# One-hot tiles of a PEER gate moved from VectorE to GpSimd, and a weight split issued earlier

## The chip, the cores and the metric

The kernel runs on one core of one Trainium2 chip. A core has a matrix engine, TensorE (PE, whose weight loads the profile lists apart as PEld), and three engines for elementwise work: VectorE (DVE), ScalarE (ACT) and GpSimd (POOL). SyncE (SP) issues most DMAs. The metric is the device time of one execution in microseconds (us), lower is better. Before the change three runs gave a median of 2891.4 us, from 2889.86 to 2892.06.

## What is computed

Two decoder blocks on 512 tokens of width 1024, all in float32. The first block is a mixer (sparse attention beside an SSD scan), a cross attention to a memory, and a PEER feed-forward; the second is another mixer and a convolutional feed-forward. The change lies at the end of the cross attention and in PEER. Cut to that:

```python
h = h + memory_cross_attention(...)          # ends with o @ w_o
af = rmsnorm(h, norm_ffn_g)
qry = (af @ w_q).reshape(n, 8, 2, 128)
s = einsum('nhpd,hpkd->nhpk', qry, sub_keys) # two sets of 128 keys per head
s_top, i_top = top_k(s, 16)
cand = s_top[:, :, 0, :, None] + s_top[:, :, 1, None, :]
sc, ci = top_k(cand, 16)
e_a, e_b = (i_top[.., 0] at ci // 16), (i_top[.., 1] at ci % 16)
experts = e_a * 128 + e_b                    # 8 x 16 of 16384 per token
gw = softmax(sc)
act = gelu(einsum('td,tkd->tk', x, u_tab[experts]))
y = einsum('tk,tkd->td', gw * act, v_tab[experts])
```

## The kernel before

Tokens lie in four tiles of 128. PE multiplies in float32 by splitting each operand into a high part in a reduced format and the rest: `wtile` (L166 to L185) loads a weight tile of 128x1024 (`raw`, on SP's queue, L173), ACT copies it rounded (`whi`, L181), DVE subtracts (`wlo`, L184), and `mms` makes three products (L195 to L197). The weight tiles go round a few shared buffers in the order in which they are asked for.

The program is written as plain loops; the Tile scheduler decides the order on each engine, and each engine then runs its list in order. A tile allocated from a pool waits until the last readers of the buffer that it takes are done.

`cross` ends with eight output projections, each added to the residual by DVE (L883). `peer_query` then splits the residual into `fs` (ACT L254, DVE L255), sums squares for the norm (`rms_acc`, DVE and POOL at L276), and makes 16 query projections with the weights `w_pq[m]` through `proj_cm`. After the second of them `normed` finishes the norm (`rms_end`: sums by PE at L284, L287 on DVE, `rstd` on POOL at L289; `rbcast`, L296, on PE). Each query is multiplied with keys, and DVE takes the top 16 of 128 (L928 to L932).

PEER treats token tile 0 and the others differently. For token tile 0 the chosen rows of `u_tab` and `v_tab` are gathered by indirect DMAs that POOL issues (`gather`, L1035) and used by DVE (`sparse_step`, L1047 and L1060). For tiles 1 to 3 every expert is computed densely by PE: `dense_u` makes u for 128 experts of each of 128 rows (L1063 on), `dense_v` sums them up, weighted by a gate matrix that is zero outside the chosen experts.

`peer_route` finds the chosen experts of one token tile (L947 to L1007, all on DVE but an Exp); with its one-hot steps `oh` at L980, L983 and L986 it maps places in the candidate list to indices, and for tiles 1 to 3 it leaves them, transposed, in `eT` (L1006). `gate_chunk` makes the gate matrix of 32 tokens in 8 blocks of four tokens. For a block DVE makes B (L1015: for each token the one-hot of its e_b, 128x512 in one operation), and A holds per token the one-hot of e_a times the weight gw. A is made token by token, j = 0 to 3: some j by two ACT operations (L1021, L1022), as the table GA = ((2, 3), (3,)) says (j = 2 and 3 in even blocks, j = 3 in odd ones), the others by one DVE operation each (L1024). PE multiplies the four pairs (L1027), ACT copies the result to `stg` (L1028), and SP stores it after eight blocks (L1030). There are 12 chunks, so 96 blocks. Each product shows as two records in the trace.

A and B are `wk` tiles, 128x512, and share the six buffers (PTMP = 6) of one pool: three blocks can be made ahead of PE. `peer` issues the work from a list with due places: the route of a token tile, its four chunks, and between them the 64 first `dense_u` (UONLY = 64) and 12 first steps of the gather path. The gathered rows go round six buffers (GB = 6).

## Time and profile before

| | |
|---|---|
| median of 3 runs | 2891.4 us (2889.86 to 2892.06) |
| profiled execution | 2889.49 us, its span 2887.8 us |
| mean granted clock of PE | 0.992 of full speed |
| PE busy | 2815.3 us, 97% of the span |
| DVE busy | 2081.4 us, 72% |
| ACT busy | 1286.3 us, 45% |
| POOL busy | 619.6 us, 21% |

The profile is that of one execution; its times count from the span's start. "Idle" in a row is the time for which an engine had nothing to run before the instruction, and behind an arrow stands what ended it. A share of busy time is an average over the whole span; what a stage could win has to be read in that stage. The gate chunks run from 1110 to about 1385 us, the last sum of the cross attention is at 915.66 us.

### The profile page before, as it was taken

What the parts mean: (1) busy time and instruction counts of PE and PEld (TensorE: products, weight loads), DVE (VectorE), ACT (ScalarE), POOL (GpSimd) and SP (SyncE); (2) the same over time, 40 slices, a digit from 0 to 9 for tenths busy, and PEclk for the clock granted to TensorE, in tenths of its full rate; (3) what the DMA queues carried; (4) which work ended last, traced back from release to release, by engine and by line L of the source; (5) the groups of instructions that cost most, each with busy time, mean ns of one, the idle gap of its engine ahead of it and who ended that gap; (6) DMA issues with size and microseconds to landing.
All of it is one profiled execution on the core that took longest, in us unless ns stands there. A gap on an engine that the chain in (4) does not pass through costs nothing.

```text
span 2887.8 us, 38487 instructions
## 1 busy us (share of the span) xinstructions
PE 2815.3 (97%) x14365; PEld 2407.0 (83%) x14365; DVE 2081.4 (72%) x3721; ACT 1286.3 (45%) x2208; POOL 619.6 (21%) x448
## 2 busy tenths in 40 slices
PE   7899999999999999999999999999999999999998
PEld 6767788888887899999988888888887778888887
DVE  7986874545556999967578787878895876564646
ACT  4256764333434337777433333333333664432322
POOL 3421330001201000000245454554550010010100
PEclk9999999999999999999999999999999999999999
DMA  4211113324423245677899999999992202223332
GB/s 132 81 52 59 52 52 95 96 87 139 138 81 99 88 133 171 207 252 249 281 341 345 332 350 337 346 339 345 334 379 73 95 30 74 88 80 101 96 95 88
DMA packets 179852, 491.98 MB, mean 170 GB/s; under 512 B 14880, under 2 KB 66336, under 8 KB 179472
## 3 DMA queue, kind: packets, MB, share of 16 engines
q1 hardware_dynamic: 142320, 353.97, 36.4%
q0 software_dynamic: 37344, 135.54, 13.4%
q8 instruction: 113, 1.85, 0.3%
q14 instruction: 75, 0.61, 0.1%
HBM read 446.39 MB, written 41.94 MB: 169 GB/s over the span
## 4 chain that ended last, share of the span: by engine, by line
PE 82%; DVE 10%; issue 4%; ACT 2%; POOL 0%; DMA 0%; DVEq 0%; POOLq 0%; ACTq 0%
PE mm L197 10%; PE mm L196 10%; PE mm L195 10%; PE acc L1106 6%; PE acc L1108 6%; PE acc L1112 6%; PE u L195 5%; PE u L196 5%; PE u L197 5%; PE mm L1027 3%; PE mm L1395 2%; PE mm L1397 2%; PE mm L1398 2%; DVE wlo L184 1%; PE sm L303 1%
## 5 line engine op out<-in xcount | busy, mean ns | idle before, releaser
L181 ACT ACTIVATE whi<-raw 128x1024 fp32r<-128x1024 f32 x498 | 526.9, 1059 | 1104.1 <-PE mm L196 348.6
L184 DVE TENSOR_TENSOR wlo<-raw,whi 128x1024 fp32r<-128x1024 f32 x476 | 614.2, 1292 | 387.1 <-ACT whi L181 325.2
L195 PE MATMUL u<-nsh,whi 128*128 128x384 f32 x1024 | 347.6, 339 | 2.7 <-ACT al L1070 2.7
L196 PE MATMUL u<-nsl,whi 128*128 128x384 f32 x1024 | 346.4, 338 | 0.0
L197 PE MATMUL u<-nsh,wlo 128*128 128x384 f32 x1024 | 345.8, 338 | 0.0
L1035 POOL DMA_INDIRECT gr<-u_tab,pidx x128 | 187.3, 1463 | 638.1 <-DVE gr L1047 253.2
L1035 POOL DMA_INDIRECT gr<-v_tab,pidx x128 | 200.2, 1564 | 193.5 <-DVE acc L1060 172.1
L1106 PE MATMUL acc<-whi,Wh 128*128 128x512 f32 x768 | 237.7, 391 | 0.0
L1108 PE MATMUL acc<-whi,Wl 128*128 128x512 f32 x768 | 237.0, 390 | 0.0
L195 PEld LDWEIGHTS u<-nsh,whi 128*128 128x128 f32 x1024 | 193.1, 189 | 5.3 <-ACT al L1070 3.0
L1112 PE MATMUL acc<-wlo,Wh 128*128 128x512 f32 x768 | 194.9, 389 | 0.0
L196 PEld LDWEIGHTS u<-nsl,whi 128*128 128x128 f32 x1024 | 193.0, 188 | 2.3
L197 PEld LDWEIGHTS u<-nsh,wlo 128*128 128x128 f32 x1024 | 192.9, 188 | 0.0
L195 PE MATMUL mm<-ah,whi 128*128 128x512 f32 x424 | 173.3, 409 | 13.4 <-ACT whi L181 13.4
L197 PE MATMUL mm<-ah,wlo 128*128 128x512 f32 x424 | 170.5, 402 | 1.4 <-DVE wlo L184 1.2
L196 PE MATMUL mm<-al,whi 128*128 128x512 f32 x424 | 170.6, 402 | 0.0
L1108 PEld LDWEIGHTS acc<-whi,Wl 128*128 128x128 f32 x768 | 144.1, 188 | 31.4
L1112 PEld LDWEIGHTS acc<-wlo,Wh 128*128 128x128 f32 x768 | 144.1, 188 | 30.0
L1106 PEld LDWEIGHTS acc<-whi,Wh 128*128 128x128 f32 x768 | 143.3, 188 | 26.3
L1060 DVE SCALAR_TENSOR_TENSOR acc<-gr,act,acc 128x1024 f32<-128x1024 f32 x127 | 163.3, 1286 | 1.6
L1047 DVE SCALAR_TENSOR_TENSOR gr<-gr,xt 128x1024 f32<-128x1024 f32 x128 | 152.4, 1219 | 0.0
L196 PE MATMUL mm<-fl,whi 128*128 128x512 f32 (+1 forms) x336 | 129.8, 387 | 0.3
(642 smaller groups left out, 6089.5 us busy)
## 6 DMA issues: line engine op xcount, KB each, us to landing
raw<-uT SPq DMA_DIRECT2D x128, 512.0 KB
raw<-v_tab SPq DMA_DIRECT2D x128, 512.0 KB
raw<-w_cm SPq DMA_DIRECT2D x61, 512.0 KB
gd<-stg SPq DMA_DIRECT2D x12, 2048.0 KB
Gl<-gd SPq DMA_DIRECT2D x32, 768.0 KB
ad<-al SPq DMA_DIRECT2D x32, 384.0 KB
al<-ad SPq DMA_DIRECT2D x16, 768.0 KB
raw<-w_fg SPq DMA_DIRECT2D x22, 512.0 KB
```

Of the source, the lines that this page charges most:

```text
L181: nc.scalar.activation(hi[:, :n], raw[:, :n], AF.Copy)
L184: self.paced = (eng or nc.vector).tensor_tensor(lo[:, :n], raw[:, :n], hi[:, :n].bitcast(F), op=OP.subtract)
L195: mm(ps, w[0][:, cs[k]], xh, start=k0 + k == ends[0], stop=False)
L196: mm(ps, w[0][:, cs[k]], xl, start=False, stop=False)
L197: mm(ps, w[1][:, cs[k]], xh, start=False, stop=k0 + k == k1)
L1027: nc.tensor.matmul(pg[:, j * 128:(j + 1) * 128], B[:, j], A[:, j], start=True, stop=True)
L1035: self.nc.gpsimd.indirect_dma_start(out=t, out_offset=None, in_=self.I[tab], in_offset=bass.IndirectOffsetOnAxis(ap=self.idx[:, j:j + 1], ...
L1047: nc.vector.scalar_tensor_tensor(u, u, 1.0, self.xt, op0=OP.mult, op1=OP.mult, accum_out=self.act0[:, i:i + 1])
L1060: nc.vector.scalar_tensor_tensor(self.acc0, v, w, self.acc0, op0=OP.mult, op1=OP.add)
L1106: mm(self.accp[tt * 2 + hf], wh[:, ts], hi[:, cs[hf]], start=first, stop=False)
L1108: mm(self.accp[tt * 2 + hf], wl[:, ts], hi[:, cs[hf]], start=False, stop=False)
L1112: mm(self.accp[tt * 2 + hf], wh[:, ts], lo[:, cs[hf]], start=False, stop=last)
```

## The change

Two edits. In `gate_chunk` the tile of j = 0 is made by GpSimd with the same operation; j = 1, and j = 2 in odd blocks, stay on VectorE. And the weight `w_pq[0]` is asked for (loaded and split) in the code of `cross`, ahead of the last addition, instead of in `peer_query`.

```diff
@@ cross
         for m in range(8):
             ps = self.proj_cm(I["w_co"][m], os)
+            if m == 7:
+                self.wq = self.wtile(I["w_pq"][0], 1024)
             nc.vector.tensor_tensor(h(m), h(m), ps, op=OP.add)
@@ peer_query
         for m in range(16):
             hd, q = divmod(m, 2)
-            ps = self.proj_cm(I["w_pq"][m], fs)
+            ps = self.proj_cm(I["w_pq"][m], fs, w=None if m else self.wq)
@@ gate_chunk
-                    nc.vector.tensor_scalar(A[:, j], self.io128, e, w, op0=OP.is_equal, op1=OP.mult)
+                    (nc.vector if j else nc.gpsimd).tensor_scalar(A[:, j], self.io128, e, w, op0=OP.is_equal, op1=OP.mult)
```

All lines behind the first edit have numbers higher by 2 in the changed kernel. The scheduler lays the work out anew. Three places of the new order:

POOL, from the preparation of PEER on, in the kernel before (`sa` and `rstd` belong to the norm):

```order
L944 MEMSET grid 128x1152
L276 TENSOR_TENSOR sa_7357<-sa_7357,sq 128x512 x3
L289 TENSOR_TENSOR rstd<-rv,mhalf 128x4
L1035 DMA gr<-u_tab,pidx 128x1024 x128
L1035 DMA gr<-v_tab,pidx 128x1024 x128
```

The same place of the changed kernel:

```order
L946 MEMSET grid 128x1152
L276 TENSOR_TENSOR sa_7363<-sa_7363,sq 128x512 x3
L289 TENSOR_TENSOR rstd<-rv,mhalf 128x4
L1026 TENSOR_SCALAR A<-io_7332,eT 128x128 x32
L1037 DMA gr<-u_tab,pidx 128x1024
L1026 TENSOR_SCALAR A<-io_7332,eT 128x128 x11
L1037 DMA gr<-u_tab,pidx 128x1024 x2
L1026 TENSOR_SCALAR A<-io_7332,eT 128x128 x8
L1037 DMA gr<-u_tab,pidx 128x1024 x2
L1026 TENSOR_SCALAR A<-io_7332,eT 128x128 x8
L1037 DMA gr<-u_tab,pidx 128x1024
L1026 TENSOR_SCALAR A<-io_7332,eT 128x128 x5
```

The gathers stood alone in the queue; now they stand among the one-hot tiles, with up to eleven of these ahead of one.

DVE, up to the fourth block of the fourth chunk (its tiles are A_9993 and B_9994), in the kernel before; `prc`, `pt8` and `oh` belong to the route of the next token tile:

```order
L972 CAST prc_11252<-pcu_11249 128x256
L974 SCALAR_TENSOR_TENSOR pt8_11254<-prc_11252 128x128
L975 TENSOR_TENSOR prc_11252<-prc_11252,pt8_11254 128x128
L976 TENSOR_TENSOR prc_11252<-prc_11252,pt8_11254 128x128
L980 TENSOR_TENSOR oh_11259<-prc_11252,io16_7324 128x2048
L1015 TENSOR_TENSOR B_9994<-io128_7326,eT_7330 128x512
L1024 TENSOR_SCALAR A_9993<-io128_7326,eT_7330 128x128 x3
L1015 TENSOR_TENSOR B_10008<-io128_7326,eT_7330 128x512
```

The same place of the changed kernel:

```order
L982 TENSOR_TENSOR oh_11259<-prc_11252,io16_7330 128x2048
L184 TENSOR_TENSOR wlo_10070<-raw_10066,whi_10068 128x1024
L184 TENSOR_TENSOR wlo_10103<-raw_10099,whi_10101 128x1024
L985 TENSOR_TENSOR oh_11259<-oh_11259,pit_11203 128x2048
L988 TENSOR_TENSOR oh_11259<-oh_11259 128x128x8
L988 TENSOR_TENSOR oh_11259<-oh_11259 128x128x4
L184 TENSOR_TENSOR wlo_10222<-raw_10218,whi_10220 128x1024
L988 TENSOR_TENSOR oh_11259<-oh_11259 128x128x2
L184 TENSOR_TENSOR wlo_10373<-raw_10369,whi_10371 128x1024
L1017 TENSOR_TENSOR B_9994<-io128_7332,eT_7336 128x512
L1026 TENSOR_SCALAR A_9993<-io128_7332,eT_7336 128x128 x2
L1017 TENSOR_TENSOR B_10008<-io128_7332,eT_7336 128x512
```

Ahead of the block there are now four weight splits and the rest of a one-hot step. Counted from the first B of the stage to this one, DVE makes 40 tiles A instead of 67, 13 splits instead of 12, and three times the steps L983 and L986 (L985 and L988 now) instead of twice; all else is the same.

PE at that block, before; the u products are those of `dense_u`:

```order
L1027 MATMUL mm_9987<-A_9978,B_9979 128x128 x4
L195 MATMUL u_10072<-nsh_7377,whi_10068 128x384
L196 MATMUL u_10072<-nsl_7378,whi_10068 128x384
L197 MATMUL u_10072<-nsh_7377,wlo_10070 128x384
L195 MATMUL u_10072<-nsh_7377,whi_10068 128x384
L196 MATMUL u_10072<-nsl_7378,whi_10068 128x384
L197 MATMUL u_10072<-nsh_7377,wlo_10070 128x384
L1027 MATMUL mm_10001<-A_9993,B_9994 128x128 x4
```

And in the changed kernel:

```order
L1029 MATMUL mm_9972<-A_9964,B_9965 128x128 x4
L1029 MATMUL mm_9987<-A_9978,B_9979 128x128 x4
L195 MATMUL u_10072<-nsh_7383,whi_10068 128x384
L1029 MATMUL mm_10001<-A_9993,B_9994 128x128 x4
L196 MATMUL u_10072<-nsl_7384,whi_10068 128x384
L1029 MATMUL mm_10016<-A_10007,B_10008 128x128 x2
```

Five of the six u products ahead of the block stand behind it now.

DVE at the last sum of the cross attention (L883, the second row of hx_62 here), before:

```order
L883 TENSOR_TENSOR hx_62<-hx_62,mm 128x512
L184 TENSOR_TENSOR wlo<-raw,whi 128x1024 x3
L883 TENSOR_TENSOR hx_62<-hx_62,mm 128x512
L341 TENSOR_SCALAR flip<-fp 128x128
L346 TENSOR_TENSOR ix<-ix,ip 128x128
```

The changed kernel, there and up to the first top-16 step (L930 now):

```order
L885 TENSOR_TENSOR hx_62<-hx_62,mm 128x512
L184 TENSOR_TENSOR wlo<-raw,whi 128x1024
L885 TENSOR_TENSOR hx_62<-hx_62,mm 128x512
L341 TENSOR_SCALAR flip<-fp 128x128
L346 TENSOR_TENSOR ix<-ix,ip 128x128
```

```order
L255 SCALAR_TENSOR_TENSOR fsl_7343<-hx_61,gcols,fsh_7341 128x512 x4
L255 SCALAR_TENSOR_TENSOR fsl_7344<-hx_62,gcols,fsh_7342 128x512 x4
L276 TENSOR_TENSOR sa_7361<-sa_7361,sq 128x512 x3
L184 TENSOR_TENSOR wlo<-raw,whi 128x1024 x2
L930 MAX rt<-psk 128x8 x2
```

Two splits left their place ahead of the last sum; one of them stands behind the sums for the norm, and the other further back.

## Rows read from the trace of the kernel before

**Rows 1.** The page: the span, and busy time, share and instructions of each engine.

```profile
span 2887.8 us, 38487 instructions
...
PE 2815.3 (97%) x14365; PEld 2407.0 (83%) x14365; DVE 2081.4 (72%) x3721; ACT 1286.3 (45%) x2208; POOL 619.6 (21%) x448
```

**Rows 2.** Stretches of time: window and its length, then each engine busy, clock, DMA share.

```profile
945.00:1040.00 95.00, 95.00 (x483) 78.68 (x482) 91.69 (x481) 37.99 (x56) 0.00 (x0) 1.00 0.27 86
1110.00:1165.00 55.00, 52.40 (x342) 50.18 (x341) 54.90 (x149) 44.28 (x96) 1.12 (x1) 1.00 0.63 200
1165.00:1210.00 45.00, 43.12 (x286) 41.79 (x285) 43.59 (x131) 31.59 (x71) 1.90 (x2) 1.00 0.62 194
1210.00:1400.00 190.00, 190.00 (x1257) 185.55 (x1257) 134.25 (x284) 144.49 (x316) 14.42 (x13) 1.00 0.78 249
```

**Rows 3.** Waits of PE, 1110 to 1210 us: total us, times, longest us.

```profile
PE mm L1027 <- DVE A L1024: 3.4, 3, 1.5
```

**Rows 4.** Timeline, first block: start us, us, engine, line, count [idle before <-releaser].

```profile
1110.08 1.24 DVE L184 TENSOR_TENSOR wlo<-raw,whi 128x1024 fp32r<-128x1024 f32 x1
...
1111.82 0.62 DVE L1024 TENSOR_SCALAR A<-io,eT 128x128 f32<-128x128 f32 x2
...
1112.24 0.63 PE L1027 MATMUL mm<-A,B 128*128 128x128 f32 x3 [1.48 <-DVE A L1024]
```

**Rows 5.** Timeline, fourth block of the fourth chunk.

```profile
1189.93 2.29 DVE L980 TENSOR_TENSOR oh<-prc,io 128x2048 bf16<-128x2048 bf16 x1
...
1190.44 0.42 PE L195 MATMUL u<-nsh,whi 128*128 128x384 f32 x1
...
1192.74 0.85 DVE L1024 TENSOR_SCALAR A<-io,eT 128x128 f32<-128x128 f32 x3
...
1193.23 0.57 PE L1027 MATMUL mm<-A,B 128*128 128x128 f32 x3 [1.50 <-DVE A L1024]
```

**Rows 6.** Instructions by line, 1110 to 1390 us: count | busy us, mean ns | idle.

```profile
L1027 PE MATMUL mm<-A,B 128*128 128x128 f32 x768 | 106.6, 280 | 4.5 <-DVE A L1024 3.4 <-ACT stg L1028 0.6 <-ACT A L1021 0.3
...
L1024 DVE TENSOR_SCALAR A<-io,eT 128x128 f32<-128x128 f32 x240 | 70.3, 346 | 0.0
...
L184 DVE TENSOR_TENSOR wlo<-raw,whi 128x1024 fp32r<-128x1024 f32 x45 | 55.0, 1224 | 40.4 <-ACT whi L181 40.3
...
L1035 POOL DMA_INDIRECT gr<-u_tab,pidx x16 | 17.4, 1090 | 424.1 <-DVE B L1015 199.7 <-DVE gr L1047 80.8 <-ACT al L1070 66.6
...
L983 DVE TENSOR_TENSOR oh<-oh,pit 128x2048 bf16<-128x2048 bf16 x4 | 4.9, 1228 | 0.0
...
L986 DVE TENSOR_TENSOR oh<-oh 128x1024 bf16<-128x1024 bf16 x4 | 2.8, 692 | 0.0
...
L986 DVE TENSOR_TENSOR oh<-oh 128x512 bf16<-128x512 bf16 x4 | 1.8, 448 | 0.0
```

**Rows 7.** Durations of the selects at L1632, all in ns.

```profile
L1632 POOL TENSOR_SCALAR_AFFINE_SELECT me<-me x32: 287/294/846, 2298.1 to 2383.9; 128x128 f32<-128x128 f32 x32
```

**Rows 8.** Instructions by line, all of POOL.

```profile
L276 POOL TENSOR_TENSOR sa<-sa,sq 128x256 f32<-128x256 f32 x3 | 2.3, 781 | 5.9 <-ACT sq L272 5.7
```

**Rows 9.** Timeline of DVE and POOL, 2341 to 2344 us.

```profile
2341.55 1.23 DVE L1505 TENSOR_TENSOR EQ<-EQ,gqk 128x1024 f32<-128x1024 f32 x1
...
2342.09 1.69 POOL L1632 TENSOR_SCALAR_AFFINE_SELECT me<-me 128x128 f32<-128x128 f32 x3 [1.16 <-ACT me L1630]
```

**Rows 10.** Timeline of DVE at the last sum of the cross attention.

```profile
912.49 2.36 DVE L184 TENSOR_TENSOR wlo<-raw,whi 128x1024 fp32r<-128x1024 f32 x2 [0.18 <-ACT whi L181]
```

**Rows 11.** Timeline of PE, norm of the first queries.

```profile
944.23 1.16 PE L296 MATMUL sm<-ident,rstd 128*128 128x128 f32 x8 [0.77 <-POOL rstd L289]
```

**Rows 12.** DMAs of 1140 to 1400 us: issue, count, median us to landing.

```profile
gr<-u_tab,pidx POOLq DMA_INDIRECT x16, 6.7
```

**Rows 13.** Timeline of POOL, one gather.

```profile
1268.33 1.15 POOL L1035 DMA_INDIRECT gr<-u_tab,pidx  x1 [10.54 <-DVE gr L1047]
```

**Rows 14.** Timeline of DVE, the use of that gather.

```profile
1303.44 1.22 DVE L1047 SCALAR_TENSOR_TENSOR gr<-gr,xt 128x1024 f32<-128x1024 f32 x1
```


## The prediction

> **What bounds the kernel now.** First the page: the span is 2887.8 us, and TensorE (PE) is busy in 2815.3 of it, VectorE (DVE) in 72%, GpSimd (POOL) in 21% [rows 1]. A change that only moves elementwise work can return no more than PE's idle time in the stretches that it touches, so I looked for that idle time next. Time by stretch [rows 2]: while the queries are made (945 to 1040) PE is busy throughout, though DVE is at 91.69 of 95. In the gate stage, which runs from 1110 to about 1385 us, PE is short of 55.00 − 52.40 = 2.60 us up to 1165 and of 45.00 − 43.12 = 1.88 us up to 1210, where DVE is full; from 1210 to 1400 it is busy 190.00 of 190, with DVE at 134.25. So the whole gate stage has about **4.5 us** to give, all of it in its first 100 us. The waits of PE there name DVE's one-hot tile A for 3.4 us, in 3 waits [rows 3]; two of them are 1.48 us at 1112.24 [rows 4] and 1.50 us at 1193.23 [rows 5].
>
> **Part 1, the 96 moved tiles.** There are 12 chunks of 8 blocks, and each block gives its j = 0 tile to POOL: 96 of the 240 tiles that DVE makes at L1024 [rows 6]. A group of three of them covers 0.85 us [rows 5] and one of two 0.62 us [rows 4], so one less is worth 0.23 us to DVE, 96 are worth 22 us. But that is DVE time, and from 1210 us on nobody waits for DVE; there the relief counts as nothing, covered by PE's products, which run without a gap. What counts is when A is ready at the stalls before 1210:
>
> - First block, 1112.24. Its A goes from two DVE tiles to one. POOL starts its tile when eT is ready, beside the split and the B tile that DVE still makes first (1.24 us at 1110.08), so POOL's tile is there in time: **−0.2** us (0 to −0.3).
> - Stall at 1193.23, the fourth block of the fourth chunk. DVE has 27 tiles fewer to make ahead of it, 27 × 0.23 = 6.2 us. But the order refills that place: one more split (1224 ns), one more one-hot product (1228 ns) and its three additions (692 and 448 ns, and I take 448 for the third too) stand ahead of B_9994 now [rows 6], together 4.0 us. Net, A is ready 2.2 us earlier. PE comes earlier as well: in the order it has one product u ahead of this block instead of six. The six ran from 1190.44 until PE fell idle at 1193.23 − 1.50 = 1191.73, 0.21 us each; five of them are 1.1 us, done after the block instead [rows 5]. The wait goes from 1.50 to 1.50 − 2.2 + 1.1 = 0.4, so **−1.1** us (−1.5 to 0).
> - The rest of the 4.5 us (4.48 − 1.48 − 1.50 = 1.5 us) lies in shorter waits in between, where the same refilling takes nearly everything: **−0.2** us (−1.5 to 0).
>
> What does one tile cost on POOL? The trace of before has no such instruction. Its nearest row has the same shape and one input: the 128x128 select at L1632, 294 ns in the median and 846 ns at most [rows 7]. Two-input arithmetic on twice the elements takes 781 ns on average [rows 8]. Beside DVE work with two inputs three selects take 1.69 us instead of 0.9, the first of them until DVE's 1.23 us operation ends [rows 9]. So one tile lies between 0.3 and 0.85 us; I take 0.4, since the select is nearest in shape and inputs, and about 0.7 where DVE makes B beside it.
>
> When would POOL hold PE up? A and B tiles share six buffers, so three blocks are made ahead and each later one is released when PE ends a block. L1027's records cover 106.6 us over 96 blocks, 1.1 us a block [rows 6]. In a bunch of eight blocks POOL makes five while PE works six, so it is late only beyond 6 × 1.1 / 5 = **1.3 us** a tile. 0.7 stays clear of that. For the odd late tile (B behind A, a gather ahead of it) I put 0.1 us on each of 8 bunches: **+0.8** us (0 to +2.4).
>
> POOL's queue also holds the indirect row gathers, now behind the tiles in a fixed order. A gather takes POOL about 1.1 us (17.4 us for 16) [rows 6] and its rows need 6.7 us more [rows 12]. In before they are early: one is issued at 1268.33 and read at 1303.44 [rows 13, 14]. In the changed order a gather stands behind as many as eleven tiles, and so behind PE's progress; most of that lead goes, but the reader stands at the start of a stretch of u products, and the splits that DVE makes behind it are a ring of four ahead of PE. I cost it at 0 and keep the case as a rival. The gathers themselves are ready to go when POOL reaches them, so no tile waits long behind one.
>
> **Part 2, the first query weight.** The order shows that this weight was already split ahead of the last sum. What moves are two other splits: the DVE operations at 912.49 (2.36 us for two) [rows 10] go behind the sums for the norm. DVE itself waited there for ScalarE's copies (0.18 us), and PE not for these two, so nothing is gained. ScalarE's two copies of these weights move too, and PE can then do one product fewer early. That would show where PE waits for POOL's rstd, at 944.23 (0.77 us) [rows 11]; a delay of the norm lengthens that wait, at worst by as much again, and one product is a small part of the norm's chain, so I take a third of it: **+0.25** us (0 to +0.8). Behind 945 the extra split is covered by PE's full stretch. The weight buffers are handed on one place further from here, and every load keeps its lead, so 0.
>
> **Sum.** −0.2 − 1.1 − 0.2 + 0.8 + 0.25 = −0.45 us on the profiled execution's 2889.49, so about 2889.0 on its scale. That execution is 1.9 us below the median of the three runs (2891.4); on the scale of the median I forecast **2890.9 us**. That is no change: about 0.2%, 5.8 us, is what a measurement of this kernel can tell. From the bounds of the terms, without a rival, −3.3 to +3.2 us around 2891.4 gives 2888 to 2895.
>
> **The rivals.**
>
> *F, all stalls go.* If DVE does come out of each block far enough ahead, all 4.5 us go: 2886.9. The order speaks against it, because it puts route work where the tiles were. Even then it is not 0.2%; faster by more needs a second source, such as a gain outside the stretches that I read, which I cannot name. Chance of faster by over 0.2%: 0.10. F within 0.2%: 0.14.
>
> *S, slower: the tile on POOL is too slow.* The mechanism: in a bunch each block needs its POOL tile, and POOL waits for DVE whenever that runs a two-input operation. B, one per block, is such. The price decides at 1.3 us a tile: at 1.5 us PE waits 5 × 1.5 − 6 × 1.1 = 0.9 us in each of 11 bunches, some 10 us (2901); at 2 us 3.4 us in each, some 37 us (2929). For it speaks the select held until DVE was through [rows 9]; against it that even then it took under 0.85 us [rows 7]. Chance 0.11. The Trainium skill ("GPSIMD Engine Reference", Specifications and Key points) says that GpSimd shares its SBUF interfaces with VectorE and contends with VectorE instructions with two SBUF inputs; the select at 2342.09 agrees in kind. In Engine selection it puts one-input work near line rate, which no run here has shown for this operation.
>
> *G, slower: late gathers.* Where gathered rows arrive after DVE reaches their use, DVE stands, at most for the 6.7 us from issue to landing [rows 12], with the splits and tiles of its queue behind it. One such wait in full passed on to PE gives 2898, two give 2905; it decides when the ring of splits has run out. For it speaks the queue order, against it the slack of the ring, which at four weights of 24 products at 0.2 us is far more than one wait. Chance 0.05.
>
> *C, a first use that is slow.* If POOL's first tile were late by x us, the first block would wait x minus the 1.5 us or so that it waits already longer, once; up to x = 7 this stays within 0.2%. The rows speak against any x that counts: of the 32 selects, the first among them, none took more than 846 ns [rows 7]. Chance 0.06. The same page (Instruction dispatch) gives about 6 us for the first call to freshly loaded code, an estimate of 4.5 us more here; no row of before shows it.
>
> My forecast, between −3 and +3 us, has the remaining 0.54.
>
> **Chances and range.** Faster by over 0.2%: 0.10. Within 0.2%: 0.54 + 0.14 + 0.06 = 0.74. Slower by over 0.2%: 0.11 + 0.05 = 0.16. The range goes from 2884 (a little past F) to 2900 (the near end of S and G), which leaves out about 2 in 10.
>
> **What would show it.** Right: POOL gets 96 tiles at L1026 of 0.3 to 0.85 us; DVE's busy time falls by 22 to 33 us (96 × 0.23 to 96 × 0.346); PE's idle from 1110 to 1210 falls from 4.5 us to 2 to 4; none arises from 1210 to 1400. Wrong: PE waits on POOL at L1029, or tiles over 1.3 us (S); idle DVE before L1049 with a DMA as releaser, and PE waiting on splits behind it (G); the first block later than 1112 by several us (C); PE idle that appears or vanishes outside 910 to 950 and 1110 to 1400 (none of my cases).

## The result

The changed kernel is slower: 2929.6 us in the median of four runs (2924.3 to 2934.7), against 2890.6 us of four runs of the kernel before on the same chip. The ratio is 1.013, with a 95% interval of [1.0118, 1.0143]. I had forecast 2890.9 us, no change, and a range of 2884 to 2900; the time lies outside, and near the 2929 us that the rival on slow GpSimd tiles gave for a tile of 2 us. The profiled execution took 2930.65 us.

The page of the changed kernel, the rows that answer to [rows 1]:

```profile
span 2928.9 us, 38580 instructions
...
PE 2828.1 (97%) x14365; PEld 2415.8 (82%) x14365; DVE 2059.9 (70%) x3625; ACT 1287.5 (44%) x2208; POOL 767.7 (26%) x544
```

DVE lost 2081.4 − 2059.9 = 21.5 us of work, the 22 us of the sum. PE's busy time rose by 12.8 us and its idle time in the span from 72.5 to 100.8 us.

The same kernel by stretches; columns as in [rows 2]:

```profile
945.00:1040.00 95.00, 95.00 (x484) 78.70 (x483) 91.37 (x481) 37.79 (x56) 0.00 (x0) 1.00 0.29 92
1110.00:1165.00 55.00, 48.06 (x307) 45.46 (x306) 50.76 (x134) 42.01 (x92) 30.19 (x19) 1.00 0.52 164
1165.00:1210.00 45.00, 41.73 (x275) 39.65 (x274) 34.70 (x102) 30.22 (x67) 18.83 (x14) 1.00 0.56 183
...
1210.00:1430.00 220.00, 199.03 (x1265) 192.55 (x1264) 124.01 (x230) 146.91 (x323) 118.17 (x79) 0.98 0.65 212
```

While the queries are made nothing changed. In the gate stage PE was short of 6.94 + 3.27 us where it had been short of 2.60 + 1.88, and from 1210 on, where it had been full, it now lacks 21 us of 220.

For a clean comparison I cut every trace at the same two instructions of PE: the first product of the gate (L1027, L1029 after the change) and the first sum over v (L1106, now L1108). Between them PE has the same 2046 or so records in every kernel of this study. I call this stretch **the stage**. The kernel before, then the changed one:

```profile
1112.20:1429.60 317.40, 314.36 (x2046) 306.68 (x2047) 244.34 (x571) 229.86 (x492) 22.66 (x20) 1.00 0.73 233
```

```profile
1113.80:1466.40 352.60, 324.10 (x2046) 313.28 (x2047) 221.74 (x472) 229.38 (x489) 167.86 (x115) 0.99 0.64 210
```

The stage went from 317.4 to 352.6 us, **35.2 of the 41 us** that the span grew by. PE's idle time in it (length less busy) went from 3.0 to 28.5 us. Ahead of the stage 1.6 us were lost (1.2 of them in the wait for its first product), and the 763.0 us of the sums over v behind it were not touched. The second decoder block added 4.4 us in this trace; of that below.

What PE waited for in the changed kernel, the row that answers to [rows 3]:

```profile
PE mm L1029 <- POOL A L1026: 28.4, 36, 2.7
PE mm L1029 <- DVE B L1017: 2.5, 3, 1.7
```

The instructions of the gate, answering to [rows 6]:

```profile
L1026 POOL TENSOR_SCALAR A<-io,eT 128x128 f32<-128x128 f32 x96 | 150.5, 1574 | 310.1 <-DVE eT L1008 183.8 <-PE mm L1029 102.9 <-DVE oh L985 12.4
...
L1029 PE MATMUL mm<-A,B 128*128 128x128 f32 x768 | 112.2, 285 | 31.2 <-POOL A L1026 28.4 <-DVE B L1017 2.5
...
L1017 DVE TENSOR_TENSOR B<-io,eT 128x512 f32<-128x512 f32 x96 | 65.9, 687 | 37.8 <-issue 26.5 <-PE mm L1029 6.8 <-POOL A L1026 4.4
...
L1026 DVE TENSOR_SCALAR A<-io,eT 128x128 f32<-128x128 f32 x144 | 47.6, 357 | 0.0
```

A tile took 1574 ns on GpSimd on average, while VectorE's own tile (357 ns, 346 before) and its B (687 ns, 690 before) are nearly as they were. All 96 tiles in one row, with the shortest, the median and the longest in ns:

```profile
L1026 POOL TENSOR_SCALAR A<-io,eT x96: 782/1404/4232, 1110.7 to 1418.9; 128x128 f32<-128x128 f32 x96
```

### The profile page after: what moved, and what is told of

It is laid out like the page before. It is cut to its first block, busy times and chain, and to the rows that moved or that the text cites. A ratio compares the mean times of both kernels' runs of the same rounds, so it can differ in the third digit from the quotient of the medians.

```text
span 2928.9 us, 38580 instructions
## 1 busy us (share of the span) xinstructions
PE 2828.1 (97%) x14365; PEld 2415.8 (82%) x14365; DVE 2059.9 (70%) x3625; ACT 1287.5 (44%) x2208; POOL 767.7 (26%) x544
## 4 chain that ended last, share of the span: by engine, by line
PE 79%; DVE 10%; issue 4%; POOL 3%; ACT 1%; DMA 0%; POOLq 0%; DVEq 0%; ACTq 0%
PE mm L196 10%; PE mm L197 10%; PE mm L195 9%; PE acc L1108 6%; PE acc L1110 6%; PE acc L1114 6%; PE u L196 5%; PE u L197 5%; PE u L195 5%; POOL A L1026 2%; PE mm L1397 2%; PE mm L1399 2%; PE mm L1400 2%; PE mm L1029 1%; DVE wlo L184 1%
## 5 line engine op out<-in xcount | busy, mean ns | idle before, releaser
L1108 PE MATMUL acc<-whi,Wh 128*128 128x512 f32 x768 | 237.7, 391 | 0.0
L1026 POOL TENSOR_SCALAR A<-io,eT 128x128 f32<-128x128 f32 x96 | 150.5, 1574 | 310.1 <-DVE eT L1008 183.8
L1049 DVE SCALAR_TENSOR_TENSOR gr<-gr,xt 128x1024 f32<-128x1024 f32 x128 | 152.4, 1219 | 22.8 <-DMA gr<-u_tab,pidx 22.8
L1108 PEld LDWEIGHTS acc<-whi,Wh 128*128 128x128 f32 x768 | 143.3, 188 | 26.3
```

The lines of the kernel that those rows point to most:

```text
L1026: (nc.vector if j else nc.gpsimd).tensor_scalar(A[:, j], self.io128, e, w, op0=OP.is_equal, op1=OP.mult)
L1049: nc.vector.scalar_tensor_tensor(u, u, 1.0, self.xt, op0=OP.mult, op1=OP.mult, accum_out=self.act0[:, i:i + 1])
L1108: mm(self.accp[tt * 2 + hf], wh[:, ts], hi[:, cs[hf]], start=first, stop=False)
```

## How a tile comes to take 1.6 us

The timeline of the changed kernel in the bunch of gate blocks at 1275 us, PE, DVE and POOL, columns as in [rows 4]:

```profile
1274.25 2.84 PE L1029 MATMUL mm<-A,B 128*128 128x128 f32 x24
...
1275.40 7.59 POOL L1026 TENSOR_SCALAR A<-io,eT 128x128 f32<-128x128 f32 x4 [10.72 <-PE mm L1029]
...
1276.51 0.69 DVE L1017 TENSOR_TENSOR B<-io,eT 128x512 f32<-128x512 f32 x1
...
1277.68 0.68 DVE L1017 TENSOR_TENSOR B<-io,eT 128x512 f32<-128x512 f32 x1
...
1277.84 1.16 PE L1029 MATMUL mm<-A,B 128*128 128x128 f32 x8 [0.58 <-POOL A L1026]
...
1278.54 0.68 DVE L1017 TENSOR_TENSOR B<-io,eT 128x512 f32<-128x512 f32 x1
...
1279.65 0.68 DVE L1017 TENSOR_TENSOR B<-io,eT 128x512 f32<-128x512 f32 x1
...
1279.77 0.71 PE L1029 MATMUL mm<-A,B 128*128 128x128 f32 x4 [0.60 <-POOL A L1026]
...
1280.51 1.21 DVE L1049 SCALAR_TENSOR_TENSOR gr<-gr,xt 128x1024 f32<-128x1024 f32 x1
...
1282.28 1.16 PE L1029 MATMUL mm<-A,B 128*128 128x128 f32 x8 [1.44 <-POOL A L1026]
```

PE has 24 records, the three blocks made ahead, in 2.84 us, 0.95 us a block. GpSimd starts its tile for the fourth block when PE ends the first, at 1275.40, and four tiles in a row take it 7.59 us, 1.9 us each. In those 7.6 us VectorE ran four operations B and a gather step, all with two tensor inputs, for 3.9 us (and before them the rest of a weight split, also with two). PE stood still three times, for 0.58, 0.60 and 1.44 us, each time for GpSimd. A tile that meets no such operation takes 0.78 to 0.81 us. One that meets a whole B takes 1.44 us, the most frequent duration in the list. So, as I read the rows, GpSimd's tile stands still while VectorE runs an operation with two inputs, and then goes on. Over all 96 tiles, two-input operations overlap GpSimd's records by 96.0 us, and these records are 75 us longer than 96 x 0.79 us: some four fifths of the overlap were lost. An operation that begins late in a tile costs little: the tile at 1412.04 takes 0.79 us, though a B begins at 1412.38.

VectorE's top-8 steps, which take one tensor, do not hold a tile. Here two tiles run beside them in 1.69 us, 0.79 us each and 0.1 us between them:

```profile
1169.67 1.69 POOL L1026 TENSOR_SCALAR A<-io,eT 128x128 f32<-128x128 f32 x2 [11.55 <-PE mm L1029]
...
1169.91 0.29 DVE L964 MAX8 psc<-grid 128x8 f32<-128x144 f32 x1
...
1170.13 0.29 DVE L967 MAX8 psc<-grid 128x8 f32<-128x144 f32 x1
```

The first block shows the same, and whether a first use costs something:

```profile
1110.43 1.23 DVE L184 TENSOR_TENSOR wlo<-raw,whi 128x1024 fp32r<-128x1024 f32 x1
...
1110.71 4.27 POOL L1026 TENSOR_SCALAR A<-io,eT 128x128 f32<-128x128 f32 x2 [166.21 <-DVE eT L1008]
...
1111.56 0.70 DVE L1017 TENSOR_TENSOR B<-io,eT 128x512 f32<-128x512 f32 x1
...
1112.42 0.70 DVE L1017 TENSOR_TENSOR B<-io,eT 128x512 f32<-128x512 f32 x1
...
1113.82 1.05 PE L1029 MATMUL mm<-A,B 128*128 128x128 f32 x7 [2.71 <-POOL A L1026]
```

The first two tiles took 4.27 us, beside a split of 1.23 us and three B of 0.70 us (two of them in these rows); PE waited 2.71 us, 1.2 us longer than in [rows 4]. What it was held by accounts for the first tile, and an excess for a first use does not show.

That is PE's idle time. The rest of the stage's loss lies in PE's busy time. The granted clock of PE fell to its lower level twice, in or behind waits for GpSimd, in a stage that ran at full clock throughout before:

```profile
1220.00:1230.00 10.00, 7.43 (x43) 7.05 (x42) 6.02 (x12) 5.71 (x16) 7.02 (x4) 0.83 0.09 37
1355.00:1370.00 15.00, 12.38 (x66) 11.99 (x67) 8.16 (x19) 8.74 (x24) 10.57 (x7) 0.77 0.33 112
```

Each slice's deficit, doubled, is its time at half clock: 0.17 x 10 x 2 and 0.23 x 15 x 2, 3.4 and 6.9 us. PE was busy in 9.5 us of that, at half the pace, so 4.7 us were lost. Idle 25.5 and clock 4.7 leave some 5.0 us; L1029's records cover 112.2 us where L1027's covered 106.6 [rows 6], and part of that is the first product after each of the 36 waits, which runs alone. I did not separate it further.

## The experiments

Sixteen more kernels were run. The table has the medians and the ratio to the kernel before on the same chip (its median beside the groups of runs was 2890.6 to 2892.7), then, from each profile, the length of the stage, PE's idle time in it, PE's wait for GpSimd's tile, and VectorE's wait for gathered rows (both with the 4 us ahead of the stage).

| run | median, us | ratio [interval] | stage | idle | tile | rows |
|---|---|---|---|---|---|---|
| before | 2890.6 | | 317.4 | 3.0 | 0 | 0 |
| the change | 2929.6 | 1.0130 [1.0118, 1.0143] | 352.6 | 28.5 | 28.4 | 22.8 |
| e1_tiles_only | 2931.2 | 1.0129 [1.0112, 1.0146] | 357.3 | 29.0 | 29.2 | 23.0 |
| e2_split_only | 2891.8 | 0.9996 [0.9986, 1.0005] | 317.4 | 3.1 | 0 | 0 |
| e3_unread | 2929.6 | 1.0134 [1.0117, 1.0151] | 358.7 | 39.2 | 0 | 43.6 |
| e4_odd_blocks | 2903.1 | 1.0041 [1.0027, 1.0055] | 330.7 | 13.5 | 7.6 | 17.9 |
| e9_before_nsp0 | 2889.0 | 0.9989 [0.9980, 0.9999] | 318.7 | 3.0 | 0 | 0 |
| e10_after_nsp0 | 2924.8 | 1.0113 [1.0093, 1.0133] | 350.7 | 24.5 | 26.2 | 0 |
| e11_unread_nsp0 | 2896.7 | 1.0012 [1.0003, 1.0022] | 320.0 | 3.8 | 0 | 0 |
| e8_first_three | 2900.7 | 1.0031 [1.0020, 1.0043] | 325.6 | 7.6 | 3.2 | 24.3 |
| e5_gb5_ptmp8 | 2912.7 | 1.0076 [1.0059, 1.0093] | 339.6 | 16.6 | 14.1 | 22.5 |
| e6_B_one_input | 2905.9 | 1.0047 [1.0032, 1.0063] | 327.4 | 8.2 | 6.5 | 19.7 |
| e6b_B_one_before | 2889.0 | 1.0000 [0.9990, 1.0009] | 317.6 | 3.7 | 0 | 0 |
| e12_first_three_nsp0 | 2902.6 | 1.0039 [1.0024, 1.0053] | 325.3 | 5.1 | 5.5 | 0 |
| e7_one_op | 2899.1 | 1.0026 [1.0016, 1.0036] | 325.9 | 6.9 | 6.2 | 20.8 |
| e15_B_one_nsp0 | 2900.8 | 1.0041 [1.0027, 1.0054] | 326.3 | 8.0 | 7.1 | 0 |
| e16_B_one_before_nsp0 | 2891.2 | 0.9997 [0.9987, 1.0007] | 318.0 | 4.4 | 0 | 0 |
| e13_second_third | 2896.7 | 1.0015 [1.0006, 1.0025] | 322.9 | 5.7 | 0.4 | 22.1 |

In the second decoder block, which no edit touches, these profiles need between 683.9 and 690.7 us from the last sum over v to PE's last product: five lie between 690.0 and 690.7 (the change, e1, e7, e11, e12), the others between 683.9 and 686.4. The changed kernel's 690.0 against 685.6 before is within that, though every engine's order is the same in both. Here is one place where the two traces differ, first the kernel before:

```profile
2269.19 0.63 PE L195 MATMUL mm<-bh,whi 128*128 128x512 f32 x1
...
2272.86 0.50 PE L197 MATMUL mm<-bh,wlo 128*128 128x512 f32 x1 [0.19 <-DVE wlo L184]
```

And the same place of the changed kernel:

```profile
2306.35 0.39 PE L196 MATMUL mm<-bl,whi 128*128 128x512 f32 x1
...
2309.64 0.50 PE L197 MATMUL mm<-bh,wlo 128*128 128x512 f32 x1 [1.77 <-DVE wlo L184]
```

PE runs at half clock (0.63 us a record instead of 0.39) just ahead of a split for which it would otherwise have to wait, in the one; in the other it arrives at full clock, waits 1.77 us, and has its half-clock stretch later. So the median of a run is blurred by some us that the stage is free of, and I argue from the stage where a few us matter.

### Which edit, and what of the tile

**e1_tiles_only and e2_split_only** take one edit each. The diffs against the kernel before:

```diff
# e1_tiles_only
-                    nc.vector.tensor_scalar(A[:, j], ...)
+                    (nc.vector if j else nc.gpsimd).tensor_scalar(A[:, j], ...)
# e2_split_only
+            if m == 7:
+                self.wq = self.wtile(I["w_pq"][0], 1024)
...
-            ps = self.proj_cm(I["w_pq"][m], fs)
+            ps = self.proj_cm(I["w_pq"][m], fs, w=None if m else self.wq)
```

> Only the 96 tiles go to GpSimd; the first query weight is split where it was before. Theory held (a tile takes 0.79 us of GpSimd alone and stands still while VectorE runs an operation with two inputs, 1.57 us on average, over the 1.3 us that the bunch allows): as slow as the whole change, 2920 to 2935 us, PE's waits for the tile near 28 us. Rival split (the moved weight split shifts every later load): most of the loss goes, under 2900.

> Only the weight split is moved; all one-hot tiles stay on VectorE. Theory held: 0 to +2 us on before (the trace of the change shows +0.57 us up to the gate stage). Rival split: at least +10 us.

The whole loss is with the tiles (1.0129 against the whole change's 1.0130), and the split alone does nothing that can be measured (0.9996, its interval spanning 1). In the changed kernel's trace PE lags behind the trace of before by 0.10 us at the first keys product and by 0.35 us at the last, 0.25 us more. That is less than these profiles scatter: in e2, with the same split, the lag grows by 2.0 us between the same products, 1.65 of them in PE's wait for `rstd` (2.42 us instead of 0.77). So a price of the split of this size is not shown.

**e4_odd_blocks** halves the number of GpSimd's tiles:

```diff
-                    (nc.vector if j else nc.gpsimd).tensor_scalar(A[:, j], ...)
+                    (nc.vector if j or q % 2 == 0 else nc.gpsimd).tensor_scalar(A[:, j], ...)
```

> The change with GpSimd making the tile in odd blocks alone, 48 instead of 96. Theory held: GpSimd has twice the time for a tile, 2.6 us in a bunch, so PE waits for it under 5 us and the time is 2888 to 2897. Rival queue (a tile is late because the row gathers stand ahead of it in GpSimd's queue, not because of its own time): waits fall only in proportion to the tiles, to about 14 us, and the time is 2905 to 2915.

```profile
PE mm L1029 <- POOL A L1026: 7.6, 13, 1.0
```

Half of the tiles cost 13.3 us of the stage, 38% of 35.2. Neither theory had it: the wait for GpSimd, 7.6 us, is over the one's 5 and under the other's 14. With tiles that now average 1665 ns GpSimd has in fact the time, but a single late tile still stops PE (in waits of at most 1.0 us; the granted clock was full in the whole stage), and VectorE still stood for gathered rows. That sent me to the gathers.

**e3_unread** leaves all tiles with VectorE and lets GpSimd make the 96 a second time:

```diff
                     nc.vector.tensor_scalar(A[:, j], ...)
+                    if j == 0:
+                        x = self.wk("xA", (128, 128), bufs=1)
+                        nc.gpsimd.tensor_scalar(x, self.io128, e, w, op0=OP.is_equal, op1=OP.mult)
```

> The kernel before, where VectorE still makes all 240 tiles, and GpSimd makes the 96 tiles a second time into a buffer that nobody reads. Theory held: GpSimd's tiles take 0.79 us alone and about 1.5 us on average, VectorE's B stays at 0.69 us, and the time stays within 4 us of before, because nobody waits for the tile. Rival port (both engines lose when they run side by side): VectorE's B and A get longer by over 0.1 us, and 10 to 30 us are lost though nobody reads the tiles.

My expectation fell: nobody reads the tiles, and still 37 us were lost, while B stayed at 0.69 us, so the rival port does not hold either. The waits of VectorE in this kernel:

```profile
DVE gr L1050 <- DMA gr<-u_tab,pidx: 43.6, 2, 22.4
```

GpSimd runs its list in order. The tiles, which nothing holds back now, were placed 32 in a row, the next 32 wait for the next token tile's eT, and behind these stand the gathers that VectorE needs before. PE and VectorE have the order of before in the stage. So the experiment measured a queue, not a port. It had to be made again without gathers.

### Without gathers in the stage

Three kernels with NSP = 0, which puts all gather steps behind the gate stage: the kernel before, the changed kernel, and the one with unread tiles.

```diff
-SP0, SP1, NSP, VSP = 32, 2.4, 12, 124
+SP0, SP1, NSP, VSP = 32, 2.4, 0, 124
```

> The kernel before with no gather step in the first stage (NSP = 0): all row gathers are issued and used after the gate stage. It is the base line for the two runs beside it; nothing waits for gathers in the gate stage of any theory, and the time is 2888 to 2900 us.

> The change without gather steps in the first stage (NSP = 0). Theory held (the price of a tile, 1.57 us, is over what the bunch allows): PE still waits 25 us or more for the tile, and it is at least 25 us slower than the base line of this call. Rival gathers (VectorE stands at gathers that GpSimd issues late behind its tiles, 22.8 us in the change, and that is what PE pays for): less than 10 us slower than that base line. If both count, between: my sum for the price alone, 11 bunches of 5 x 1.57 - 6 x 1.1 = 1.25 us, is 14 us.

> GpSimd makes the 96 tiles a second time, unread, and there are no gather steps in the first stage (NSP = 0). The run with the unread tiles lost 37 us, in two waits of VectorE of some 22 us for gathered rows. Rival gathers: without gathers the loss is gone, within 4 us of the base line of this call. Rival port: at least 10 us are lost still, and VectorE's B or A takes over 0.1 us longer.

The stage of the base line, and of the changed kernel without gathers:

```profile
1112.70:1431.40 318.70, 315.68 (x2046) 306.25 (x2047) 231.43 (x549) 231.51 (x492) 10.51 (x9) 1.00 0.66 212
```

```profile
1115.70:1466.40 350.70, 326.19 (x2047) 314.15 (x2048) 208.69 (x450) 229.99 (x488) 150.81 (x104) 0.98 0.59 192
```

What PE waits for in the latter:

```profile
PE mm L1029 <- POOL A L1026: 26.2, 38, 2.9
```

The change costs 350.7 − 318.7 = 32.0 us of the stage where no gather stands in it, against 35.2 with gathers. That is at least 25, as the price of the tile demanded; some 3 us are left for the gathers, though VectorE stands 22.8 us for them.

With the tiles unread and no gathers the stage is 320.0 us, 1.3 over its base line, and PE and VectorE have the same order in both. The rows of the gate, first with the tiles, then of the base line:

```profile
L1027 POOL TENSOR_SCALAR xA<-io,eT 128x128 f32<-128x128 f32 x96 | 134.3, 1399 | 264.8 <-DVE eT L1006 255.5
...
L1024 DVE TENSOR_SCALAR A<-io,eT 128x128 f32<-128x128 f32 x240 | 71.9, 353 | 0.0
L1015 DVE TENSOR_TENSOR B<-io,eT 128x512 f32<-128x512 f32 x96 | 65.7, 685 | 1.5 <-PE mm L1030 0.8
```

```profile
L1024 DVE TENSOR_SCALAR A<-io,eT 128x128 f32<-128x128 f32 x240 | 70.1, 345 | 0.0
L1015 DVE TENSOR_TENSOR B<-io,eT 128x512 f32<-128x512 f32 x96 | 66.1, 688 | 1.5 <-PE mm L1027 0.8
```

GpSimd's tiles take 1.4 us beside VectorE; VectorE's B takes 685 instead of 688 ns and its A 353 instead of 345. So VectorE hardly pays (96 x 3 ns less and 240 x 8 ns more, 1.6 us of its time); nearly the whole hold falls on GpSimd. The median of this run lies 7.7 us over its base line's, which is over the 4 us that I had allowed and under the 10 of the rival port. Between the two profiled executions, 7.6 us apart, 1.3 us lie in the stage and 5.1 us in the second block, in which the profiles scatter by as much.

### Own time and hold

**e6_B_one_input** takes away the two-input operation that meets every tile. B is made by four operations with one tensor input each; **e6b_B_one_before** does the same to the kernel before.

```diff
-            nc.vector.tensor_tensor(B, self.io128[:, None, :].to_broadcast([128, 4, 128]),
-                                    self.eT[:, 1, t0:t0 + 4][:, :, None].to_broadcast([128, 4, 128]), op=OP.is_equal)
+            for j in range(4):
+                nc.vector.tensor_scalar(B[:, j], self.io128, self.eT[:, 1, t0 + j:t0 + j + 1], None, op0=OP.is_equal)
```

> The change with VectorE's tile B made by four operations with one tensor input (128x128 each) instead of one with two inputs (128x512). Theory hold (GpSimd stands still only while VectorE runs a two-input operation): tiles beside B take about 0.8 us instead of 1.44, PE's waits for GpSimd fall from 28 us to under 12; VectorE has 4 x 0.26 - 0.69 = 0.35 us more to do for each block, and what that costs is read beside the next run. Rival always slow (GpSimd is slowed by any work of VectorE): tiles stay at 1.4 us or more and the waits stay over 20 us.

> The kernel before with B made by four one-input operations: the base line for the run above. All theories: VectorE has about 34 us more to do in the gate stage, hidden where PE is full; 2890 to 2905 us.

```profile
L1026 POOL TENSOR_SCALAR A<-io,eT 128x128 f32<-128x128 f32 x96 | 111.8, 1170 | 320.9 <-DVE eT L1008 182.6 <-ACT whi L181 60.9 <-PE mm L1029 51.2
...
L1018 DVE TENSOR_SCALAR B<-io,eT 128x128 f32<-128x128 f32 x384 | 87.3, 290 | 4.8 <-issue 4.1 <-PE mm L1029 0.2
```

```profile
PE mm L1029 <- POOL A L1026: 6.5, 17, 1.6
```

The tiles fall to 1170 ns on average, and PE's wait for them from 28.4 to 6.5 us. VectorE is not idler in this kernel (its four B operations cover 87.3 us instead of 65.9), so it is the kind of VectorE's work that holds GpSimd, and not its amount, that counts most. Most tiles beside one-input work take 0.9 to 1.1 us, 1.00 us on average over the 70 that meet no two-input operation: over 0.79, and not the 0.8 that I had expected. With the base line's stage at 317.6 us the change still costs 9.8 us here.

**e15_B_one_nsp0** and its base line **e16_B_one_before_nsp0** ask whether these 9.8 us are gathers; they are the two kernels with NSP = 0.

> The change with B made by one-input operations and without gather steps in the first stage. With B alone changed the stage from the first gate product to the first sum over v lasted 327.4 us against 317.6 of its base line. Theory gathers (what was left there, 9.8 us, is VectorE standing 19.7 us at late gathers): the stage is within 4 us of its base line in the run beside it. Theory own time (GpSimd's 0.9 to 1.1 us a tile are too slow by themselves): 8 us or more over it.

> The kernel before with B made by one-input operations and without gather steps in the first stage: the base line of the run above. 2886 to 2896 us by either theory, the stage 316 to 320 us.

```profile
PE mm L1029 <- POOL A L1026: 7.1, 22, 1.6
```

326.3 − 318.0 = 8.3 us: the gathers explain 1.5 of the 9.8. The rest I put down to GpSimd's own time, at 0.9 to 1.1 us a tile about PE's pace in a bunch, and to the tiles that still meet a split or a route step; what the new order of the work costs by itself (see e13 below) is in it too, and these runs do not part the two.

**e7_one_op** makes the tile cheaper by itself. In these 96 tiles the multiplication by the weight is left out.

```diff
-                    (nc.vector if j else nc.gpsimd).tensor_scalar(A[:, j], self.io128, e, w, op0=OP.is_equal, op1=OP.mult)
+                    if j:
+                        nc.vector.tensor_scalar(A[:, j], self.io128, e, w, op0=OP.is_equal, op1=OP.mult)
+                    else:
+                        nc.gpsimd.tensor_scalar(A[:, j], self.io128, e, None, op0=OP.is_equal)
```

> GpSimd makes its tile with the comparison alone; the multiplication by the weight is left out in these 96 tiles, so the gate of every fourth token is wrong by its weights. Theory per operation (the 0.79 us that a tile takes alone come from its two operations): a tile takes 0.4 to 0.6 us alone, the stage gets shorter by 10 us or more than with the change. Theory per element (the time is that of passing over 128 columns, whatever is done to them): 0.7 to 0.8 us alone still, and the time stays within 5 us of the change, 2922 to 2935 us.

```profile
L1029 POOL TENSOR_SCALAR A<-io,eT x96: 596/1140/3007, 1112.3 to 1393.6; 128x128 f32<-128x128 f32 x96
```

The shortest tile falls from 782 to 596 ns: the second operation costs 0.19 us of the 0.78, and the time is not that of passing over the elements alone. The stage falls from 352.6 to 325.9 us. Taking 0.19 us from each tile (and 0.35 us on average, 1574 to 1223 ns, since a shorter tile meets less of VectorE's work) gives back 26.7 of 35.2 us. That is how steep the loss is near the pace at which PE takes tiles. All four engines run the stage in the order of the changed kernel here, so the 26.7 us are due to the duration of the tile alone, and what the new order costs lies within the other 8.5 us.

### Slack instead of price

**e5_gb5_ptmp8** lets four blocks be made ahead instead of three. Room for it comes from one gather buffer.

```diff
-GB, PTMP, VMB = 6, 6, 11
+GB, PTMP, VMB = 5, 8, 11
```

> The change with eight buffers for A and B instead of six, so four blocks are made ahead; to make room the gathered rows have five buffers instead of six. Theory price (in a bunch of eight blocks GpSimd's tiles at about 1.65 us cannot follow PE's 0.9 us a block, and what is made ahead is all that helps): one tile less inside the bunch, PE's waits for GpSimd fall from 28 us to 10 to 18, the time to 2905 to 2918. Rival gathers: nothing gets better, or it gets worse with fewer gather buffers, 2925 or more.

```profile
PE mm L1029 <- POOL A L1026: 14.1, 15, 2.9
```

Within what the price demanded: the wait halves, and the stage falls by 13 us, with one gather buffer less.

**e8_first_three** gives GpSimd the tiles of the first three blocks of a chunk alone, **e12_first_three_nsp0** the same without gathers in the stage, and **e13_second_third** those of the second and third block.

```diff
# e8, e12
-                    (nc.vector if j else nc.gpsimd).tensor_scalar(A[:, j], ...)
+                    (nc.vector if j or q > 2 else nc.gpsimd).tensor_scalar(A[:, j], ...)
# e13
+                    (nc.vector if j or q not in (1, 2) else nc.gpsimd).tensor_scalar(A[:, j], ...)
```

> The change with GpSimd's tile in the first three blocks of each chunk alone, 36 tiles, which the six buffers let it make ahead while PE multiplies for u. Theory held: there is time enough, PE waits under 3 us for GpSimd's tile, and the time is within 4 us of before. Rival gathers: VectorE still stands 10 us or more at late gathers, and the time is 8 us or more over before.

> GpSimd's tile in the first three blocks of each chunk alone, and no gather steps in the first stage (NSP = 0). Theory price and gathers together: the first three blocks have time, and without gathers behind the tiles nothing else is late, so PE waits less than the 4.5 us of before in the gate stage, 2884 to 2892 us. Rival price alone (the 9 us that the first three blocks lost come from the tiles, not from the gathers): 2896 or more.

> GpSimd's tile in the second and third block of each chunk alone, 24 tiles. With the first three blocks the loss was 8 us of the stage, and PE's longest waits for GpSimd, 2.9 and 0.3 us or so, were at a first block, where a tile held by VectorE's work took 3 us. Theory hold: without the first blocks these waits go and the stage is within 3 us of before, 2888 to 2896 us in all. Rival gathers: GpSimd's queue is still mixed with tiles, VectorE stands at late gathers, and 6 us or more are lost.

The waits of PE in the last of them:

```profile
PE mm L1029 <- DVE A L1026: 4.1, 4, 1.7
...
PE mm L1029 <- POOL A L1026: 0.4, 2, 0.2
```

Three misses. In e8 the numbers of the rival came true, 24.3 us of late gathers and 9.0 us in the median; but the first three blocks lost 8.2 us of the stage with gathers and 6.6 without (325.3 − 318.7), so it is not the gathers, against my expectation for e12. Of these, 4.6 and 2.1 us are idle time. The clock accounts for the rest: PE worked 6.8 us at half clock in e8's stage (0.66 granted from 1114 to 1119 and from 1244 to 1249) and 9.5 us in e12's (0.66 from 1115 to 1125 and from 1220 to 1225), 3.4 and 4.8 us lost. In both PE also waits 2.9 us for the very first tile, which is ahead of the stage as I cut it, and e12 has one more wait of 2.6 us for a tile inside. Without the first blocks PE waits 0.4 us for GpSimd, as the hold demanded, and yet the stage is 5.5 us over before: 2.7 us are idle time, mostly small waits for VectorE and ScalarE that the new order of VectorE's work brings, and PE ran 3.4 us at half clock (0.72 and 0.94 granted in two slices of 5 us), 1.7 us lost. Where the last microsecond of it lies I have not settled. What can be said is that no share of the tiles that I gave to GpSimd paid: even with 24 of them and 0.4 us of waits for it the kernel is not faster than before (1.0015 [1.0006, 1.0025]). No kernel with tiles on GpSimd beats the kernel before. The lowest ratio is that of e9, a base line, 0.9989 [0.9980, 0.9999], nearer to 1 than the 0.2% that I take a measurement to tell, and its stage is 1.3 us longer.

## Why the prediction was wrong

**What bounds the kernel: right.** PE is the bound, and the gate stage had about 4.5 us to give. VectorE's 21.5 us were bought for nothing, as the sum had it.

**The price of a tile: the step that failed.** "So one tile lies between 0.3 and 0.85 us; I take 0.4, since the select is nearest in shape and inputs, and about 0.7 where DVE makes B beside it." A tile takes 0.78 us alone and 1.57 us on average. In the sum it stands behind the +0.8 us (0 to +2.4) for the odd late tile; measured were 28.4 us of waits for GpSimd's tile. Two things went wrong in that sentence. The own time was taken from the select at the wrong end: the tile does two operations with two scalars per partition, and by e7 each counts; 0.78 us was inside the bounds. And the upper end was no bound. 0.85 us was the longest select, and I took the hold to be in it. But [rows 9] showed how to do the sum: a select was held until VectorE's operation was through, so the hold is *added* to the own time. Every block has a B of 0.69 us, and own time and one B give 0.78 + 0.69 = 1.47 us (the trace shows 1.44), with the select's 0.29 us still 0.98 us. Splits of 1.22 us and one-hot steps of 2.28 us come on top, and they stand where a bunch begins.

**The threshold: the form right, the number too kind.** POOL, I wrote, "is late only beyond 6 × 1.1 / 5 = 1.3 us a tile". The 1.1 us a block came from the cover of L1027's records with all interruptions; in a bunch PE takes a block in 0.95 us, so the threshold is 6 x 0.95 / 5 = 1.14 us. With 1.574 us a tile, 5 x 1.574 − 6 x 0.95 = 2.2 us a bunch, 24 us in 11 bunches; measured were 28.4 us in 36 waits, since the tiles of a bunch are the held ones (1.9 us at 1275). And I had priced PE's stalls at their idle time alone; half-clock stretches and what I did not separate added 9.7 us to 25.5.

**The rival on slow tiles: the mechanism right, its chance far too low.** It named the place (PE at L1029 waiting on POOL), the cause (VectorE's two-input work) and the number at 2 us, 2929. That the time came out so near this number is luck: the tile took 1.57 us, for which the rival's own formula gives 11 x (5 x 1.574 − 6 x 1.1) = 14 us, 2905; PE's faster pace, the longer tiles inside the bunches and the 9.7 us beside the idle time made up the difference. I gave it 0.11, on the ground that even the held select took under 0.85 us; that ground was the failed step. The page "GPSIMD Engine Reference" of the Trainium skill (Specifications) says that GpSimd shares its SBUF interfaces with VectorE and contends with VectorE instructions that have two SBUF inputs. The runs agree: 0.79 us alone, 1.44 beside a B with two inputs, 0.9 to 1.1 beside a B with one. It should have had the weight of a term of the sum.

**The stalls at 1112 and 1193: overtaken.** What stood at the first block grew by 1.2 us instead of shrinking by 0.2. At the fourth block of the fourth chunk PE waits 0.57 us instead of 1.50, but for GpSimd, and three more waits for it follow in the same bunch. In e7, which has the same order and a shorter tile, this wait is

```profile
1196.33 1.16 PE L1032 MATMUL mm<-A,B 128*128 128x128 f32 x8 [0.38 <-ACT A L1024]
```

so the 0.4 us that the sum left of it was about right, though not with VectorE as the cause: GpSimd's and ScalarE's tiles end last, 0.06 us apart.

**The gathers: right in the sum, wrong in the margin.** They cost some 3 of the 35.2 us (e10; 1.5 and 1.6 in the pairs e6 and e15, e8 and e12), as "I cost it at 0" nearly had it, though the slack did go and VectorE stood 22.8 us. e3 shows what happens when the queue gets worse: with 32 unread tiles ahead of a gather 37 us are lost, of which, without gathers, 1.3 us of the stage are left (e11). The rival, to which I gave 0.05, was nearer than that chance says.

**The first use: right; the split: open.** No excess shows at the first tile. The +0.25 us of the split agree with one trace, but the traces scatter by more, and the median of e2 shows nothing of it.

## What to carry to other kernels

Before an operation is moved to GpSimd, add to its own time the time of every two-input VectorE operation that it will meet, because it stands still for nearly that long (four fifths of the overlap here), and compare the sum with the pace at which the consumer takes the results, not with GpSimd's idle share. VectorE's relief is worth only what some engine waits for, and a queue in order (GpSimd's, with its gathers) turns a late tile into late data for others. Where a buffer ring sets how far ahead work is made, the stage loses steeply once the price crosses the pace: here 0.35 us less a tile gave back three quarters of the loss.

## What I had not expected of the hardware

- The hold is one-sided and nearly whole. GpSimd's 128x128 tile goes from 0.79 to 1.44 us beside one B of 0.69 us, and up to 4.23 us beside several two-input operations, while VectorE's B stays at 685 to 688 ns (e11 against e9).
- The second operation in the same instruction costs GpSimd 0.19 us on 128x128 (782 against 596 ns, e7); on VectorE the same instruction with both takes 0.34 us.
- A stall of PE can have a tail. In the stage 25.5 us more idle time came with 9.7 us of further loss, half of it at the lower granted clock (0.77 of full speed from 1355 to 1370, 0.83 from 1220 to 1230), in a stage that ran at full clock before. Not every stall has one: e4 idled 10.4 us more in its stage, at full clock throughout.
- In the second block, unchanged and in the same order, the profiles scatter by 6.8 us (683.9 to 690.7), with the half-clock stretches at other places; a gain or loss of that size needs the stage, not the total.
